# Encoder block: the operands of 336 products of 256 columns placed 64 bytes apart modulo 128

## The chip, the cores and the metric

The kernel runs on one core of one Trainium2 chip. The metric is the device time of one execution in microseconds (us); the time before is 1156.95 us, the median of three runs (1156.94 to 1157.06). Times inside an execution come from one profiled execution of the same program.

The engines that matter here are TensorE (PE in the profile; its weight loads are shown apart, as PEld), ScalarE (ACT), VectorE (DVE), GpSimd (POOL) and the queue that issues the DMAs of weights (SP). A TensorE product has a stationary operand (here always 128x128), which a weight load brings into the array, and a moving operand, whose columns are then streamed through it. Both lie in SBUF, on-chip memory of 128 partitions; "a tile begins at byte b" means byte b of every partition.

## The reference

One layer of an encoder for 256 tokens of width 2048, all in float32:

```
h = rms_norm(x, g_mix);  proj = h @ w_in          # 512 + 256 + 64 latents, and 3 x 1024 for diff attention
q = rms_norm(c_q) @ w_uq;  kv = rms_norm(c_kv) @ w_ukv          # MLA, 8 heads of 128 + 64 (rotary)
out_mla  = softmax((q_nope k_nope + q_rope k_rope) * scale) v
out_diff = rms_norm((softmax(q1 k1) - lam * softmax(q2 k2)) v)   # 4 heads, v of 256
x = x + concat(out_mla, out_diff) @ w_out
x = x + cross_attention(x, mem) @ w_xo                           # 4 heads, 256 memory tokens
x = x + (silu(hf @ w_gate) * (hf @ w_up)) @ w_down               # hidden 5632
return rms_norm(x, g_final)
```

## The kernel before

**Products in three.** Each float32 operand is held as two float32r tiles, `h` (the value rounded, written by ScalarE, line 99) and `l` (the rest, by VectorE, line 100). `mm` (lines 89 to 93) issues three products into one PSUM accumulator: h with h (line 91), h with l (92), l with h (93). In the profile the name behind the arrow lists moving and stationary operand, such as `acc<-wh,x0T_h`; buffer numbers are left out, and all three lines are shared by all products of the kernel.

**Most products have 512 columns.** A weight piece of 1 MB comes by DMA into `wraw`, is split by ScalarE and VectorE into `wh` and `wl` (4 buffers each, line 137), and is the moving operand, with a 128x128 block of the activations as the stationary one. The feed-forward part works on pairs of blocks (`wide_project`, line 680): some pairs as plain products, some as sums of blocks with seven products instead of eight; there `t24`, the last sum, has split buffers of its own, `wh2` and `wl2`, in the pool `wsum`.

**Products of 256 columns** stand in these places:

| place | moving | stationary | products |
|---|---|---|---|
| `qT`, MLA's queries by head (`stationary`, line 405, called at 427) | `cqT` | `wh`, `wl` | 96 |
| `kT`, MLA's keys by head (line 431) | `lat` | `wh`, `wl` | 48 |
| `psc`, scores of all three attentions (`scores`, line 435) | activations | activations | 168 |
| `po`, MLA's output (`heads_out`, line 477) | `pT`, the transposed probabilities | `val` | 48 |
| `po` of cross-attention (line 628) | `pxT` | `val` | 24 |
| `pod`, diff attention's output (line 531) | `val` | `pT` | 48 |
| last 512 columns of the output, in two halves (`last_mm`, line 889): k-tiles 0 to 7 | `wh`, `wl` | `hT`, `hT2`, `forms` | 96 |
| the same, k-tiles 8 to 15 (line 893) | `w_h`, `w_l`: tiles of the pool `act` | the same | 96 |

**Where the tiles lie.** The pools are stacked in the order in which they are opened, and each tile is rounded up to 32 bytes. Worked out from the tiles' sizes, `wp` (3 `wraw` of 8192 bytes, then 4 `wh` and 4 `wl` of 4096 each) begins at byte 38,400, `act` (24 tiles of 4096: all activations that are operands) at 95,744, `sb` at 194,048, `small` at 209,408 and, when the position tables are freed, `soft` at 211,200. `soft` holds `e` (the exponentials, 4 buffers of 2048), then `pT_h` and `pT_l` (2 buffers of 2048 each). `wsum` takes the place of `soft` for the feed-forward part. All these are multiples of 128, and so the moving operand of every float32r product, and the stationary operand of every one, begins at a multiple of 128 bytes. The identity matrix of the transposes lies 96 bytes past a multiple of 128 (byte 17,248). Lines 445 to 447 put the negated maxima of a softmax in `nm`, 4 buffers of 8 bytes in `small`.

**The order of the work** on each engine comes from a planner that plays the program through with a timeline of its own (line 1002); only the DMAs of weights are kept in the order of the program. Line 895 names the pool of the last weights: from the piece with k-tile 8 on they go to tiles of `act`, so that they can be ready ahead of time.

Of the kernel before, what the change touches and what calls it, by code (L numbers as in the profile page):

```python
# [11 lines left out]
F32 = mybir.dt.float32  # L12
F32R = mybir.dt.float32r
# [6 lines left out]
P = 128  # L20
S = 256
NT = S // P
# [52 lines left out]
def encoder_block(ctx: ExitStack, tc: tile.TileContext, a, out):  # L75
# [3 lines left out]
    wp = ctx.enter_context(tc.tile_pool(name="wp", bufs=3))  # L79
    act = ctx.enter_context(tc.tile_pool(name="act", bufs=24))  # L80
    sb = ctx.enter_context(tc.tile_pool(name="sb", bufs=2))
    small = ctx.enter_context(tc.tile_pool(name="small", bufs=4))
# [27 lines left out]
            act.tile(list(shape), F32R, name=name + "_l", tag="act"),  # L110
        )

    def weights(src, fine=False, pool=None, before_k=None, cut=None, raw=None):

        nk, ncols = src.shape[1:]
        begun = raw is not None
        if not begun:  # L120
            raw = wp.tile([P, 2048], F32, name="wraw", tag="wraw", bufs=3)
        raw = raw[:, :nk * ncols].rearrange("p (k c) -> p k c", k=nk)
        step = 1 if fine else nk
        for k in range(0, nk, step):
            if before_k is not None:
                before_k(k)
            if begun and k == 0:
                continue
            tc.keep_in_program_order(nc.sync.dma_start(out=raw[:, k:k + step, :], in_=src[:, k:k + step, :]))
        ks = []  # L130
        step = max(1, 1024 // ncols // 2 * 2)
        for k in range(0, nk, step):
            n = min(step, nk - k)
            if pool:
                w = pool((P, n, ncols), "w")
            else:
                w = [wp.tile([P, 1024], F32R, name=x, tag=x, bufs=4)[:, :n * ncols].rearrange("p (k c) -> p k c", k=n)
                     for x in ("wh", "wl")]
                w = Split(*w)
            if fine:  # L140
                for j in range(n):
                    for c in ([slice(0, ncols)] if cut is None or k + j else [slice(0, cut), slice(cut, ncols)]):
                        split_into(w[:, j, c], raw[:, k + j, c])
            else:
                split_into(w, raw[:, k:k + n, :])
            ks += [w[:, j, :] for j in range(n)]
        return ks
# [18 lines left out]
    def nat(name):  # L166
        return sb.tile([P, 512], F32, name=name, tag="nat", bufs=7)

    def ps_tile(name):
        return pps.tile([P, 512], F32, name=name, tag="ps")  # L170
# [73 lines left out]
    for i in range(8):  # L244
# [10 lines left out]
        for k, w in enumerate(weights(a["w_in_lat"][i], i == 0, before_k=x0T.load_one if i == 0 else None,  # L255
                                      cut=QL if i == 0 else None, raw=lat_raw if i == 0 else None)):
            xk = x0T(2 * i + k)
            for tt in range(NT):
                x = xk[:, tt * P:(tt + 1) * P]
# [77 lines left out]
    cqT = act_tile(name="cqT")  # L337
    lat = act_tile(name="lat")
    ckvT, krT = lat[:, 0:2, :], lat[:, 2:4, :]
# [45 lines left out]
    soft = soft_pool.enter_context(tc.tile_pool(name="soft", bufs=2))  # L385
# [19 lines left out]
    def stationary(wk, xT, nk, name):  # L405

        t = act_tile(name=name)
        for hp in range(2):
            ps = ps_tile(name)
            for j in range(2):  # L410
                h = hp * 2 + j
                for kt in range(nk):
                    mm(ps[:, j * S:(j + 1) * S], wk[kt][:, h * P:(h + 1) * P], xT[:, kt, :],
                       kt == 0, kt == nk - 1)
            split_into(t[:, 2 * hp:2 * hp + 2, :], ps.rearrange("p (j t) -> p j t", j=2))
        return t
# [7 lines left out]
        qrs.append(qr)  # L424
    qT, kT, vv = [], [], []
    for hg in range(2):
        qT.append(stationary(weights(a["w_uq_n"][hg]), cqT, 4, "qT"))
        if hg == 0:
            for tt in range(NT):
                transposed(qrT, qrs[tt], tt, 4)  # L430
        kT.append(stationary(weights(a["w_ukv_k"][hg]), ckvT, 2, "kT"))
        vv.append(values(project(lambda kt: ckvT[:, kt, :], [a["w_ukv_v"][hg]])))
    mla_split = last_split[0]

# [7 lines left out]

    def softmax_parts(ps, scale):

        nm = small.tile([P, NT], F32, name="nm", tag="nm", bufs=4)
        nc.vector.tensor_reduce(out=nm, in_=ps, axis=AX.X, op=ALU.max, negate=True)
        nc.vector.tensor_scalar(out=nm, in0=nm, scalar1=scale, scalar2=None, op0=ALU.mult)
        e = soft.tile([P, NT, S], F32, name="e", tag="e", bufs=4)
        ssum = small.tile([P, NT], F32, name="ssum", tag="ssum", bufs=4)
        for tt in range(NT):  # L450
            nc.scalar.activation(e[:, tt, :], ps[:, tt, :], AF.Exp, bias=nm[:, tt:tt + 1], scale=scale,
                                 accum_out=ssum[:, tt:tt + 1])
        r = small.tile([P, NT], F32, name="rs", tag="rs", bufs=4)
        nc.vector.reciprocal(out=r, in_=ssum)
        return e, r
# [128 lines left out]
    for tt in range(NT):  # L584
        n = nat("xk")
# [30 lines left out]
    for tt in range(NT):  # L616
        n = nat("xq")
# [25 lines left out]
    def w_tile(n=2, pool=None):  # L643

        pool, tags, bufs = (wp, ("wh", "wl"), 4) if pool is None else (pool, ("wh2", "wl2"), 1)
        return Split(*[pool.tile([P, 1024], F32R, name=x, tag=x, bufs=bufs)[:, :n * 512].rearrange(
            "p (b c) -> p b c", b=n) for x in tags])

    def split_blocks(src, pool=None):
# [200 lines left out]
    for gi, (chunks, order) in enumerate(groups):  # L850
# [6 lines left out]
        src = [a["w_dn"][h, pair0:pair0 + len(hp)] for h in range(2)]  # L857
# [18 lines left out]
        for oc in (2, 3):  # L876
            pieces = [a["w_down"][c, oc - 2] for c in range(len(hp) // 2)]
            if oc == 2:
                add_out(project(xT, pieces), oc)
                for tt in range(NT):  # L880
                    final(tt, oc)
                continue

            accs = [(pacc.tile([P, 512], F32, name="acc", tag="acc"), ps_tile("acc2")) for _ in range(NT)]
            n = 4 * len(pieces) - 6
            kt = 0
            ws = []

            def last_mm(tt, h, kt, w, stop):
                mm(accs[tt][h][:, :256], xT(kt)[tt], w[:, h * 256:(h + 1) * 256], kt == 0, stop)  # L890

            for p in pieces:
                for w in weights(p, pool=act_tile if kt + 4 > n else None):
                    if kt < n:
                        for tt in range(NT):
                            for h in range(2):
                                last_mm(tt, h, kt, w, False)
                    else:
                        ws.append(w)
                    kt += 1  # L900
            for tt in range(NT):
                for h in range(2):
                    for i, w in enumerate(ws):
                        last_mm(tt, h, n + i, w, i == len(ws) - 1)
                    xs = x_res[tt][:, oc * 512 + h * 256:oc * 512 + (h + 1) * 256]
                    nc.vector.tensor_tensor(out=xs, in0=xs, in1=accs[tt][h][:, :256], op=ALU.add)
                    if h == 0:
                        meansq(xs, fss[:, tt, 3:4], 256, D)
                        nc.vector.tensor_tensor(out=xs, in0=xs, in1=gfb[1][:, 512:768], op=ALU.mult)
                        nc.vector.reduce_sum(out=fss[:, tt, 5:6], in_=fss[:, tt, 0:5], axis=AX.X)  # L910
                        continue
                    sq = nat("sq")[:, :256]
                    nc.vector.tensor_tensor_reduce(out=sq, in0=xs, in1=xs, scale=1.0 / D, scalar=fss[:, tt, 5:6],
                                                   op0=ALU.mult, op1=ALU.add, accum_out=fss[:, tt, 6:7])
                rf = small.tile([P, 1], F32, name="rf", tag="rf")
                nc.gpsimd.tensor_tensor(out=rf, in0=fss[:, tt, 6:7], in1=mhalf[:, :1], op=ALU.pow)
                xr, orow = x_res[tt], out[tt * P:(tt + 1) * P, :]
                nc.vector.tensor_scalar(out=xr[:, :384], in0=xr[:, :384], scalar1=rf, scalar2=None, op0=ALU.mult)
                nc.sync.dma_start(out=orow[:, :384], in_=xr[:, :384])
                nc.scalar.activation(xr[:, 384:1152], xr[:, 384:1152], AF.Copy, scale=rf)  # L920
                nc.scalar.dma_start(out=orow[:, 384:1152], in_=xr[:, 384:1152])
                nc.vector.scalar_tensor_tensor(out=xs, in0=xs, scalar=rf, in1=gfb[1][:, 768:1024],
                                               op0=ALU.mult, op1=ALU.mult)
                nc.vector.tensor_scalar(out=xr[:, 1152:1792], in0=xr[:, 1152:1792], scalar1=rf, scalar2=None,
                                        op0=ALU.mult)
                nc.sync.dma_start(out=orow[:, 1152:], in_=xr[:, 1152:])
# [79 lines left out]
```

## Time and profile before

| | |
|---|---|
| median of three runs | 1156.95 us |
| the profiled execution | 1157.2 us, of which 1155.4 us are the span from the first to the last instruction |
| granted TensorE clock, mean | 0.998 of full speed |
| VectorE busy | 901.2 us (78%) |
| ScalarE busy | 611.4 us (53%) |
| GpSimd busy | 69.3 us (6%) |
| DMA | 222.13 MB, 192 GB/s |

How to read it: a matmul's duration in the profile runs from its first read until its result stands in PSUM, so successive ones overlap; what a product costs in a dense stretch is the distance from its start to the start of the next one, its spacing. A row of the timeline has start, duration (both us), engine, line, operation, output and operands with shapes, and the count; idle time ahead of an instruction stands in brackets with what ended it. A row of a group ends in count, busy us and the mean in ns.

### The profile page before, as it was taken

The numbers are of one execution on the slowest core, as the hardware profiler recorded it, in microseconds if no ns is written. First come the engines' busy times: TensorE is split into PE (matmuls) and PEld (weight loads), VectorE is DVE, ScalarE is ACT, GpSimd is POOL, SyncE is SP. The second block draws the span as 40 slices with busy tenths as digits, with TensorE's granted clock in tenths as the row PEclk, the third lists the DMA queues.
The fourth block names the chain that finished last, engine by engine and source line by source line (L and its number), as shares of the span: only waits on it lengthen the run. The fifth ranks groups of instructions, "written<-read, shape, count | busy, mean of one in ns | idle before, by whom it ended". The sixth has DMA issues, their size and how long they took to land.

```text
span 1155.4 us, 14401 instructions
## 1 busy us (share of the span) xinstructions
PE 1145.1 (99%) x5510; PEld 960.9 (83%) x5510; DVE 901.2 (78%) x1197; ACT 611.4 (53%) x863; POOL 69.3 (6%) x81
## 2 busy tenths in 40 slices
PE   9999999999999999999999999999999999999997
PEld 7888888888888888888888888888888888888887
DVE  6688766586867776978888787797888788798873
ACT  6755454554665555655445554554544554554552
POOL 4920000001000000000000000000000000000021
PEclk9999999999999999999999999999999999999999
DMA  9655334445754445565555555645556555555551
GB/s 343 227 207 189 126 132 165 178 146 193 283 215 173 155 146 182 182 219 182 183 198 203 193 182 207 219 169 195 192 182 222 209 183 202 195 220 204 212 202 73
DMA packets 33764, 222.13 MB, mean 192 GB/s; under 512 B 4128, under 2 KB 4896, under 8 KB 8992
## 3 DMA queue, kind: packets, MB, share of 16 engines
q1 hardware_dynamic: 32256, 216.86, 52.2%
q0 software_dynamic: 864, 3.15, 0.8%
q10 hardware_dynamic: 576, 1.21, 0.3%
q8 instruction: 43, 0.70, 0.2%
q14 instruction: 25, 0.20, 0.1%
HBM read 219.11 MB, written 2.10 MB: 191 GB/s over the span
## 4 chain that ended last, share of the span: by engine, by line
PE 98%; DMA 0%; issue 0%; DVE 0%; ACT 0%; SPq 0%; POOLq 0%; POOL 0%; DVEq 0%; ACTq 0%
PE acc L91 28%; PE acc L92 28%; PE acc L93 28%; PE q L91 2%; PE q L92 2%; PE q L93 2%; PE pt L315 2%; PE ppt L462 1%; PE psc L92 1%; PE psc L93 1%; PE psc L91 1%; DMA wraw<-in_w_in_lat 0%; PE acckv L91 0%; PE acckv L93 0%; PE acckv L92 0%; PE pt L838 0%
## 5 line engine op out<-in xcount | busy, mean ns | idle before, releaser
L99 ACT CAST wh<-wraw 128x1024 fp32r<-128x1024 f32 (+2 forms) x399 | 399.6, 1013 | 384.4 <-PE acc L93 348.0
L100 DVE TENSOR_TENSOR wl<-wraw,wh 128x1024 fp32r<-128x1024 f32 (+2 forms) x399 | 469.0, 1184 | 166.8 <-ACT wh L99 164.9
L92 PE MATMUL acc<-wl,x2n_h 128*128 128x512 f32 x480 | 185.3, 390 | 0.0
L93 PE MATMUL acc<-wh,x2n_l 128*128 128x512 f32 x480 | 185.2, 389 | 0.0
L91 PE MATMUL acc<-wh,x2n_h 128*128 128x512 f32 x480 | 160.2, 390 | 0.0
L93 PEld LDWEIGHTS acc<-wh,x2n_l 128*128 128x128 f32 x480 | 90.1, 188 | 18.7
L91 PEld LDWEIGHTS acc<-wh,x2n_h 128*128 128x128 f32 x480 | 90.1, 188 | 18.6
L92 PEld LDWEIGHTS acc<-wl,x2n_h 128*128 128x128 f32 x480 | 90.1, 188 | 18.5
L92 PE MATMUL acc<-wl,hT_h 128*128 128x512 f32 (+1 forms) x272 | 103.7, 381 | 0.0
L93 PE MATMUL acc<-wh,hT_l 128*128 128x512 f32 (+1 forms) x272 | 103.5, 380 | 0.0
L91 PE MATMUL acc<-wh,hT_h 128*128 128x512 f32 (+1 forms) x272 | 89.3, 382 | 0.0
L91 PE MATMUL acc<-wh,x0T_h 128*128 128x512 f32 x224 | 87.1, 394 | 1.6 <-ACT wh L99 0.9
L92 PE MATMUL acc<-wl,x0T_h 128*128 128x512 f32 x224 | 88.1, 394 | 0.1
L93 PE MATMUL acc<-wh,x0T_l 128*128 128x512 f32 x224 | 87.8, 393 | 0.0
L99 ACT CAST wh<-tsum 128x1024 fp32r<-128x1024 f32 x56 | 58.3, 1049 | 42.2 <-DVE tsum L712 31.1
L100 DVE TENSOR_TENSOR wl<-tsum,wh 128x1024 fp32r<-128x1024 f32 x56 | 67.9, 1220 | 9.0 <-ACT wh L99 9.0
L91 PEld LDWEIGHTS acc<-wh,hT_h 128*128 128x128 f32 x272 | 51.2, 188 | 9.8 <-issue 0.3
L93 PEld LDWEIGHTS acc<-wh,hT_l 128*128 128x128 f32 x272 | 51.2, 188 | 9.6
L92 PEld LDWEIGHTS acc<-wl,hT_h 128*128 128x128 f32 x272 | 51.2, 188 | 9.4
L91 PEld LDWEIGHTS acc<-wh,x0T_h 128*128 128x128 f32 x224 | 42.0, 188 | 10.4 <-ACT x0T_h L102 1.3
L92 PEld LDWEIGHTS acc<-wl,x0T_h 128*128 128x128 f32 x224 | 42.0, 188 | 8.2 <-DVE wl L100 0.8
L93 PEld LDWEIGHTS acc<-wh,x0T_l 128*128 128x128 f32 x224 | 42.2, 188 | 7.5
(363 smaller groups left out, 2004.8 us busy)
## 6 DMA issues: line engine op xcount, KB each, us to landing
wraw<-in_w_gu SPq DMA_DIRECT2D x80, 1024.0 KB, 4.8
wraw<-in_w_dn SPq DMA_DIRECT2D x36, 1024.0 KB, 4.8
wraw<-in_w_in SPq DMA_DIRECT2D x24, 1024.0 KB, 4.8
wraw<-in_w_out SPq DMA_DIRECT2D x16, 1024.0 KB, 4.8
wraw<-in_w_down SPq DMA_DIRECT2D x8, 1024.0 KB, 4.8
wraw<-in_w_in_lat SPq DMA_DIRECT2D x7, 832.0 KB, 7.3
wraw<-in_w_xk SPq DMA_DIRECT2D x4, 1024.0 KB, 5.7
wraw<-in_w_xq SPq DMA_DIRECT2D x4, 1024.0 KB, 4.7
```

Source lines behind the costliest of these rows:

```text
L91: nc.tensor.matmul(o, l.h, r.h, start=start, stop=False)
L92: nc.tensor.matmul(o, l.h, r.l, start=False, stop=False)
L93: nc.tensor.matmul(o, l.l, r.h, start=False, stop=stop)
L99: last_cast[0] = nc.scalar.copy(out=dst.h, in_=src).ins
L100: last_split[0] = nc.vector.tensor_tensor(out=dst.l, in0=src, in1=dst.h.bitcast(F32), op=ALU.subtract).ins
L315: nc.tensor.transpose(out=pt[:, j * P:(j + 1) * P], in_=src[:, j * P:(j + 1) * P], identity=ident)
L462: nc.tensor.transpose(out=pt[:, kt * S + tt * P:kt * S + (tt + 1) * P], in_=p[:, tt, kt * P:(kt + 1) * P], identity=ident)
```

## The change

Four edits; no instruction is added or taken away.

1. `weights` takes a new argument `skip`. The tiles `wh` and `wl` are 1056 elements long (4224 bytes, 33 times 128) instead of 1024, and the split weights begin `skip` elements into them. The same tiles in `w_tile` (and `wh2`, `wl2` there) become as long, and are used from their first element.
2. The weights for `qT` and `kT` have `skip=16`: they begin 64 bytes into their tile.
3. So have the weights of the last 512 columns, as far as they are in `wh` and `wl` (k-tiles 0 to 7). The weights in tiles of `act` (k-tiles 8 to 15) begin where they did.
4. `nm` moves from `small` to `soft`, and has 6 buffers instead of 4. Rounded up, these take 192 bytes (64 more than a multiple of 128) at the head of `soft`, ahead of `e` and `pT`.

The pools then begin at bytes 38,400 (`wp`), 96,768 (`act`), 195,072 (`sb`), 210,432 (`small`) and 212,096 (`soft`, `wsum`), all multiples of 128; `e` and `pT` begin 64 bytes past one. In the 336 products of `qT`, `kT`, MLA's `po`, `pod` and the k-tiles 0 to 7 of the last columns, moving and stationary operand are 64 bytes apart modulo 128. The other 288 products of 256 columns, and those of 512, keep both at multiples of 128.

```diff
-    def weights(src, fine=False, pool=None, before_k=None, cut=None, raw=None):
+    def weights(src, fine=False, pool=None, before_k=None, cut=None, raw=None, skip=0):
...
-                w = [wp.tile([P, 1024], F32R, name=x, tag=x, bufs=4)[:, :n * ncols].rearrange("p (k c) -> p k c", k=n)
-                     for x in ("wh", "wl")]
+                w = [wp.tile([P, 1056], F32R, name=x, tag=x, bufs=4)[:, skip:skip + n * ncols].rearrange(
+                    "p (k c) -> p k c", k=n) for x in ("wh", "wl")]
...
-        qT.append(stationary(weights(a["w_uq_n"][hg]), cqT, 4, "qT"))
+        qT.append(stationary(weights(a["w_uq_n"][hg], skip=16), cqT, 4, "qT"))
...
-        kT.append(stationary(weights(a["w_ukv_k"][hg]), ckvT, 2, "kT"))
+        kT.append(stationary(weights(a["w_ukv_k"][hg], skip=16), ckvT, 2, "kT"))
...
-        nm = small.tile([P, NT], F32, name="nm", tag="nm", bufs=4)
+        nm = soft.tile([P, NT], F32, name="nm", tag="nm", bufs=6)
...
-        return Split(*[pool.tile([P, 1024], F32R, name=x, tag=x, bufs=bufs)[:, :n * 512].rearrange(
+        return Split(*[pool.tile([P, 1056], F32R, name=x, tag=x, bufs=bufs)[:, :n * 512].rearrange(
...
-                for w in weights(p, pool=act_tile if kt + 4 > n else None):
+                for w in weights(p, pool=act_tile if kt + 4 > n else None, skip=16):
```

## The prediction

> **What bounds the kernel now.** The page first: how much of the span each engine is busy, and which engine carries the chain of work that ended last. Then the waits, to see who waits for whom.
>
> ```profile
> span 1155.4 us, 14401 instructions
> PE 1145.1 (99%) x5510; PEld 960.9 (83%) x5510; DVE 901.2 (78%) x1197; ACT 611.4 (53%) x863; POOL 69.3 (6%) x81
> PE 98%; DMA 0%; issue 0%; DVE 0%; ACT 0%; SPq 0%; POOLq 0%; POOL 0%; DVEq 0%; ACTq 0%
> ```
> ```profile
> ACT wh L99 <- PE acc L93: 359.1, 221, 7.0
> DVE nm L446 <- PE psc L93: 4.3, 4, 1.9
> ```
>
> PE is busy for 99% of the span and is 98% of the chain. ScalarE, which makes the weights, waits 359 us in total for PE to free a buffer; the supply is ahead of the products, so a product that takes less time should move what follows it forward. The change touches the spacing of products of 256 columns alone. The timeline of PE around the last columns shows that spacing beside the one at 512 columns, without a wait between them:
>
> ```profile
> 1102.06 0.39 PE L92 MATMUL acc<-wl,hT_h 128*128 128x512 f32 x1
> ...
> 1124.73 0.39 PE L93 MATMUL acc<-wh,forms_l 128*128 128x512 f32 x1
> 1124.95 0.28 PE L91 MATMUL acc<-wh,hT_h 128*128 128x256 f32 x1
> ...
> 1136.47 0.28 PE L91 MATMUL acc<-w_h,hT_h 128*128 128x256 f32 x1
> ```
>
> From 1102.06 to 1124.95 start 101 products of 512 columns: 22.89 / 101 = 226.6 ns each. From 1124.95 to 1136.47 start the 96 of 256 columns whose weights are in `wh` and `wl`: 11.52 / 96 = 120.0 ns. At the pace of the wide ones, 256 columns would take 113.3 ns. So a narrow product takes 6.7 ns more than its columns ask for. At both widths one load of 128x128 weights belongs to each product; with 256 columns it has half the time beside which to run. I take the 6.7 ns for what the load costs when it and the moving operand read the memory in step, both from a multiple of 128 bytes.
>
> **Part by part: the 336 products.** MLA's stage and the diff attention, in the same view, with the groups for the counts (one of the three lines of each):
>
> ```profile
> 72.54 0.28 PE L91 MATMUL qT<-cqT_h,wh 128*128 128x256 f32 x1
> ...
> 78.30 0.63 PE L91 MATMUL acc<-wh,lat_h 128*128 128x512 f32 x2
> ...
> 90.60 0.28 PE L91 MATMUL kT<-lat_h,wh 128*128 128x256 f32 x1
> ...
> 93.48 0.40 PE L91 MATMUL acc<-wh,lat_h 128*128 128x512 f32 x1
> ...
> 213.55 0.28 PE L91 MATMUL pod<-val_h,pT_h 128*128 128x256 f32 x1
> 213.66 0.28 PE L92 MATMUL pod<-val_l,pT_h 128*128 128x256 f32 x1
> 213.78 0.40 PE L92 MATMUL acc<-wl,x0T_h 128*128 128x512 f32 x1
> ...
> 214.71 0.28 PE L93 MATMUL pod<-val_h,pT_l 128*128 128x256 f32 x1
> ...
> 215.90 0.40 PE L93 MATMUL acc<-wh,x0T_l 128*128 128x512 f32 x1
> ```
> ```profile
> L91 PE MATMUL qT<-cqT_h,wh 128*128 128x256 f32 x32 | 9.1, 284 | 0.0
> L91 PE MATMUL kT<-lat_h,wh 128*128 128x256 f32 x16 | 4.6, 288 | 0.0
> L91 PE MATMUL po<-pT_h,val_h 128*128 128x256 f32 x16 | 4.6, 286 | 0.0
> L91 PE MATMUL pod<-val_h,pT_h 128*128 128x256 f32 x16 | 4.5, 280 | 0.0
> ```
>
> - `qT`: 48 products from 72.54 to 78.30, 120.0 ns; three lines of 32 make 96 products, 96 x 6.7 = 0.64 us.
> - `kT`: 24 from 90.60 to 93.48, 120.0 ns; 48 products, 0.32 us.
> - The last columns: 96 products, 0.64 us.
> - `pod`: ten from 214.71 to 215.90, 119 ns; 48 products, 48 x 5.7 = 0.27 us.
> - MLA's `po`: 48 products, which stand between scores and transposes. For them I take the 0.12 us that the chain gives them (next fence); 48 x 6.7 = 0.32 us.
>
> Together 2.19 us. Less goes to two things: a product that follows one of 512 columns starts its successor after 0.11 us already (213.55 to 213.66), in some 15 places, 0.1 us; and a few `po` wait for their probabilities and gain nothing, about 0.1 us. That leaves 2.0 us. The unknown is the spacing that the new place gives. Nothing in the trace shows a float32r product with its operands 64 bytes apart. The nearest rows for the lower bound are transposes:
>
> ```profile
> 119.22 0.12 PE po L93
> ...
> 400.06 1.75 PE ppt L462 x16
> ```
>
> Sixteen in 1.75 us, 109.4 ns each, with a load of 128x128 for each, and the identity that moves lies 96 bytes past a multiple of 128, its load at one. So a load can be done in 109.4 ns when the operands are not in step: the gain can reach 288 x 10.6 + 48 x 9.6 = 3.5 us. At the other end a phase can be worse than this one. After the two `pod` at 213.55 four products of 512 columns take from 213.78 to 214.71, 232.5 ns each instead of 226.6: a step out of the steady rhythm costs 5.9 ns there, and 336 x 5.9 = 2.0 us would be lost. I take 113.3 ns, the pace of the wide products, which the first narrow ones of a run already show: between the ends it is what this kernel's own float32r products reach.
>
> The Trainium skill speaks against this reading: TensorE: Matmul & The Clock Gate (Part 2, What happens when you issue a matmul) says that moving operand and weight load have independent read ports and that loading the next weights takes no read bandwidth from the running matmul. By it the operands' places do nothing and the time stays at 1156.95 us; the trace has 6.7 ns per narrow product that the columns don't explain, but cannot say that the places cause them.
>
> **What else moves.** The order of reads behind it must hold, so I look at what feeds the faster stretches. Busy time by stretch (length, then PE, PEld, DVE, ACT):
>
> ```profile
> 72.54:78.30 5.76, 5.76 (x50) 5.75 (x49) 5.76 (x14) 2.24 (x3) 0.00 (x0) 1.00 0.39 136
> 81.85:93.48 11.63, 11.63 (x100) 11.63 (x99) 9.48 (x14) 9.35 (x15) 1.47 (x2) 1.00 0.77 273
> 1124.95:1136.47 11.52, 11.52 (x98) 11.51 (x96) 6.80 (x6) 4.29 (x7) 4.39 (x2) 1.00 0.10 40
> ```
> ```profile
> 75.70 1.22 DVE L100 TENSOR_TENSOR wl<-wraw,wh 128x1024 fp32r<-128x1024 f32 x1
> ...
> 78.79 2.36 DVE L100 TENSOR_TENSOR wl<-wraw,wh 128x1024 fp32r<-128x1024 f32 x2
> ```
>
> During the first `qT` DVE is full (5.76 of 5.76 us). Its next weights are ready at 76.92, and PE asks for them at 78.30, which becomes 77.98: 1.06 us are left. Those after that are ready at 81.15; PE begins `kT` at 81.85, which becomes 81.53: 0.38 us are left. If that cover were gone, at most the 0.32 us of the first `qT` would be lost. In the other stretches DVE and ACT have 2 us and more to spare.
>
> ScalarE and VectorE write the same elements 64 bytes later: nothing, and PE's 359 us of lead cover it if not. `nm` with six buffers can only take a wait away, and its reductions wait for PE's scores alone (4.3 us, above): nothing. No instruction and no DMA is added, and no queue is passed. `e` lies 64 bytes later too, as the stationary operand of 64 transposes; the identity is then 32 instead of 96 bytes off, as far from step as before: nothing, with 64 x 6.7 = 0.4 us either way as its bounds. The planner, which does not see addresses, sees other buffers for `nm` alone; a swap of neighbours in the softmax is worth tenths of a us.
>
> The sum: 1157.2 us of the profiled execution (1155.4 of span and 1.8 around it) less 2.0 is 1155.2. The median lies 0.25 below the profiled execution, so the forecast is 1156.95 - 2.0 = **1155.0 us** (rounded).
>
> **The rivals.**
> - *No load cost remains at all.* The 336 go to the transposes' 109.4 ns, 3.5 us less: 1153.4 us. For it: the shortest spacing in the trace has operands out of step. Against it: the wide products keep 226.6 ns although their load has twice the time, so about 0.44 ns a column seems to be the stream's own pace. The skill's formula on the same page (section Back-to-back issue gap) gives N / 2.4 + 2.5 ns, 109.2 ns at 256 columns, the same as here; at 512 it gives 215.7, which the trace's 226.6 does not reach.
> - *The places don't matter.* The load with its hand-over is itself 120 ns long for float32r, and a narrow product is bound by it: 1156.95 us. For it: PEld is busy for 11.51 of the 11.52 us of the last stretch. Against it: the transposes' loads.
> - *The new phase is worse.* With 64 bytes between them load and stream meet later in each product, and the spacing settles above 120 ns, as the wide ones do at 232.5 after a disturbance: 336 x 5.9 = 2.0 us more, and with 8 ns or more, as much as 2.7: 1159.0 to 1159.7 us. It decides from 120 ns on: every ns above is 0.34 us. Against it: those 232.5 ns are passing, not steady.
> - *The wide products suffer.* Buffers of 4224 bytes put two of four `wh` and `wl` 128 bytes off a multiple of 256 from the activations. If 128 were not the whole of the pattern, half of some 4400 wide products (5510 matmuls on the page, less 624 narrow ones, 96 of 320 columns and the transposes) could take 232.5 ns: 2200 x 5.9 = 13 us, 1170 us. Against it, a stretch where the sum `t24`, in `wsum`, has its operands 256 bytes off a multiple of 512:
>
> ```profile
> 740.63 0.39 PE L91 MATMUL q<-wh,forms_h 128*128 128x512 f32 x1
> ...
> 742.67 0.84 PE L91 MATMUL acc<-wh,x2n_h 128*128 128x512 f32 x3
> ```
>
> Nine products in 2.04 us, 226.7 ns: the larger offset is free, though not the same one.
>
> **How the numbers follow.** 0.2% is 2.3 us, about what a measurement can tell from no change: faster means below 1154.6, slower above 1159.3. The chances: forecast 0.50 (its own range 1154.3 to 1155.8, from 6.7 ns a product give or take two), no load cost 0.15, places without effect 0.22, worse phase 0.08, wide products 0.05. The range leaves out the two slow cases and the far end of the best one, some 0.18: from 1153.2 to 1157.6 us. Faster: the second case and two fifths of the first, 0.35. Slower: the wide products, half of the worse phase and a remainder for the order of work, 0.11. Same: the rest, 0.54.
>
> **What would show it.** Right: the 96 products of the last columns take 10.9 us instead of 11.52, at 113 to 114 ns, while the 96 after them stay at 120.0; `qT` goes from 5.76 to 5.45 us for 48; the scores stay at 120; 512 columns stay at 226.6. Wrong in size: a spacing near 109 or 117. Wrong in mechanism: 120.0 in the last columns, or the same gain in products that did not move. The forecast fails if the wide products leave 226.6 ns, or if gaps open in front of `kT`, where the cover is thinnest.

## The result, and the profile after

| | before | changed |
|---|---|---|
| median | 1156.95 us | 1171.46 us (1170.71 to 1172.34) |
| the profiled execution's span | 1155.4 us | 1168.9 us |

The ratio is 1.0125, with a 95% interval of 1.011 to 1.0139: the change makes the kernel 14.5 us slower. The forecast was 1155.0 us, with a range of 1153.2 to 1157.6 us; it came out near the 1170 us of the fourth rival, to which the prediction gave 0.05.

The page of the changed kernel, the same three lines, and the wait that shows whether the supply still leads:

```profile
span 1168.9 us, 14401 instructions
PE 1159.8 (99%) x5510; PEld 960.3 (82%) x5510; DVE 902.0 (77%) x1197; ACT 610.9 (52%) x863; POOL 68.2 (6%) x81
PE 98%; issue 0%; DMA 0%; DVE 0%; ACT 0%; POOLq 0%; POOL 0%; DVEq 0%; ACTq 0%
```
```profile
ACT wh L99 <- PE acc L93: 374.1, 223, 7.2
```

Nothing has taken PE's place. PE is busy for 14.7 us more with the same 5510 matmuls, and the other engines have the same work as before (DVE 902.0 instead of 901.2 us). ScalarE waits longer for PE, 374 instead of 359 us: the supply leads by more. The instructions stand in the same order on every engine as before. So the products themselves are slower, and the timeline of PE around the last columns, at the same instructions that the prediction quotes, says which (start and duration in us first):

```profile
1115.61 0.40 PE L92 MATMUL acc<-wl,hT_h 128*128 128x512 f32 x1
...
1138.88 0.28 PE L91 MATMUL acc<-wh,hT_h 128*128 128x256 f32 x1
...
1149.99 0.28 PE L91 MATMUL acc<-w_h,hT_h 128*128 128x256 f32 x1
```

The 101 products of 512 columns (the wide ones, from here on) take 23.27 us, 230.4 ns each instead of 226.6. The 96 narrow ones that were moved take 11.11 us, 115.7 ns instead of 120.0: they did become faster. Joined with the place of each operand in memory, which the program fixes, the starts in the trace give for the whole kernel:

| product, distance of the moving from the stationary operand modulo 256 | before | changed |
|---|---|---|
| 512 columns, 0 | 227.2 ns (all) | 229.6 ns (some 2160) |
| 512 columns, 128 | none | 232.0 ns (some 2190) |
| `qT`, `kT` | 120 | 113 to 115 |
| last columns, 64 / 192 | 120 | 117.8 / 113.6 |
| MLA's `po`, `pod` | 119, 118 | 118.5, 117 |

(Means without waits.) The wide ones at 128 cost 2190 x 4.8 ns = 10.5 us, and the wide ones at 0, whose operands are as far apart as before, 2160 x 2.35 ns = 5.1 us more. The narrow ones give back 1.1 us. The sum, 14.5 us, is nearly the 14.7 us that PE is busy longer; the span grew by 13.5, since PE waited about 1 us less ahead of its first products of `x0T` in this execution (0.4 instead of 1.6 us).

Why those at 0 lose too can be read where the buffers alternate, at the end of the same stretch. The twelve products from 1133.35 to 1136.09 have their operands 0 apart, the twelve from there to 1138.88 have them 128 apart:

```profile
1133.35 0.39 PE L91 MATMUL acc<-wh,hT_h 128*128 128x512 f32 x1
...
1134.05 0.39 PE L91 MATMUL acc<-wh,hT_h 128*128 128x512 f32 x1
...
1136.09 0.40 PE L91 MATMUL acc<-wh,forms_h 128*128 128x512 f32 x1
```

The first three at 0 take 0.70 us, 233 ns each; the other nine take 2.04 us, 226.7 ns, the pace of the kernel before. So after a switch from 128 to 0 a few products stay slow before the pace is back. The twelve at 128 take 2.79 us, 232.5 ns each.

### The profile page after: what moved, and what is told of

Read it like the earlier page. It is cut to its first block, busy times and chain, and to the rows that moved or that the text cites. A ratio compares the mean times of both kernels' runs of the same rounds, so it can differ in the third digit from the quotient of the medians.

```text
span 1168.9 us, 14401 instructions
## 1 busy us (share of the span) xinstructions
PE 1159.8 (99%) x5510; PEld 960.3 (82%) x5510; DVE 902.0 (77%) x1197; ACT 610.9 (52%) x863; POOL 68.2 (6%) x81
## 4 chain that ended last, share of the span: by engine, by line
PE 98%; issue 0%; DMA 0%; DVE 0%; ACT 0%; POOLq 0%; POOL 0%; DVEq 0%; ACTq 0%
PE acc L91 28%; PE acc L92 28%; PE acc L93 28%; PE q L91 2%; PE q L93 2%; PE q L92 2%; PE pt L318 2%; PE ppt L465 1%; PE psc L93 1%; PE psc L91 1%; PE psc L92 1%; PE acckv L91 0%; PE acckv L92 0%; PE acckv L93 0%; PE pt L841 0%
```

## Experiments

Theory A: the wide products have a best distance of their operands, 0 modulo 256, and the buffers of 4224 bytes took half of them off it; those that stay at 0 are slowed by the neighbours that were moved. Theory B: the narrow products in their new rhythm leave the wide ones out of step. Theory C: not the distance, but the moving operand's own place counts. Each experiment stands beside runs of the kernel before on the same chip. None leaves out any work of the kernel, and every engine's instructions have the kernel's order, but for some neighbours (10 of PE's) in those with shared buffers.

**1. The narrow products alone.** `h` and `l` share a buffer that is a multiple of 256 bytes long:

```diff
-                w = [wp.tile([P, 1056], F32R, name=x, tag=x, bufs=4)[:, skip:skip + n * ncols].rearrange(
-                    "p (k c) -> p k c", k=n) for x in ("wh", "wl")]
+                t = wp.tile([P, 2112], F32R, name="wh", tag="wh", bufs=4)
+                w = [t[:, c:c + n * ncols].rearrange("p (k c) -> p k c", k=n) for c in (skip, 1024 + skip)]
...
-    first = small.tile([P, 25], F32, name="first", bufs=1)[:, :1]
+    first = small.tile([P, 57], F32, name="first", bufs=1)[:, :1]
```

(`w_tile` likewise with offsets 0 and 1024; the longer `first` brings `soft` and `wsum` to a multiple of 256.)

> The change with one thing altered: wh and wl share buffers of 8448 bytes, 33 times 256, so that the operands of every wide product stay a multiple of 256 bytes apart, while the same 336 narrow products are 64 apart. Theory A (the distance modulo 256 sets the pace of the wide products: 0 is free, 128 costs): the wide ones are back at 226.7 ns and the narrow gain stands alone, 1154.9 to 1155.2 us. Theory B (the narrow products, once they run at 114 ns, leave the wide ones out of step, whatever the places of these): 1169 to 1172 us. Theory C (the place of the moving operand by itself, modulo 256, sets the pace): as A here, 1155.

Measured: 1156.04 us beside 1156.68, ratio 0.9996 (0.9987 to 1.0005). The same three rows of the timeline:

```profile
1101.04 0.39 PE L92 MATMUL acc<-wh,hT_h 128*128 128x512 f32 x1
...
1123.93 0.28 PE L91 MATMUL acc<-wh,hT_h 128*128 128x256 f32 x1
...
1135.24 0.29 PE L91 MATMUL acc<-w_h,hT_h 128*128 128x256 f32 x1
```

The wide ones are back at 226.6 ns (22.89 / 101), while the narrow ones are at 117.8 ns (11.31 / 96). B falls: 336 faster narrow products disturb nothing. But the gain is 0.6 us in the medians, not 2, and no more than the measurement can tell from none. (All 336 are still 64 apart modulo 128, but modulo 256 not all are where the change has them: with these buffers the last columns are all at 64 and `qT` and `kT` all at 192, where the change has half of each.)

**2. The longer buffers alone.** The kernel before, with `[P, 1056]` for `[P, 1024]` in `weights`, and in `w_tile` for the pool `wp`.

> The kernel before with wh and wl in buffers of 4224 bytes and nothing else: no weights 64 bytes later, nm where it was. Theory A: half of the wide products are 128 off a multiple of 256, the narrow ones gain nothing: what the change costs plus the 2 us that its narrow products gain, 1172 to 1174 us. Theory B: nothing is out of step, 1156.9 us. Theory C: as A, since the moving operands of half the wide products begin at 128 modulo 256.

Measured: 1171.26 us beside 1156.68, ratio 1.0129 (1.0115 to 1.0143).

```profile
1115.79 0.40 PE L92 MATMUL acc<-wl,hT_h 128*128 128x512 f32 x1
...
1139.06 0.28 PE L91 MATMUL acc<-wh,hT_h 128*128 128x256 f32 x1
```

230.4 ns for the wide products (23.27 / 101), as after the whole change. The 128 bytes that each buffer was lengthened by are the whole loss; B is out.

**3 and 4. All distances, or all places.** The activations 128 bytes later, by a tile in a pool of its own ahead of `act`; then weights and activations alike 128 bytes later, by a longer tile in `const`:

```diff
+    padp = ctx.enter_context(tc.tile_pool(name="padp", bufs=1))
     act = ctx.enter_context(tc.tile_pool(name="act", bufs=24))
...
-    first = small.tile([P, 25], F32, name="first", bufs=1)[:, :1]
+    first = padp.tile([P, 32], F32, name="first")[:, :1]
```
```diff
-    mhalf = const.tile([P, 8], F32, name="mhalf")
+    mhalf = const.tile([P, 40], F32, name="mhalf")[:, :8]
```

> The kernel before with the pool of the activations 128 bytes later and wh, wl and all else where they were: every wide product has its operands 128 apart modulo 256, and none moves its moving operand. Theory A: all of some 4400 wide products take 5.4 ns more, as those 128 apart do after the change: about 1181 us. Theory B: 1156.9 us. Theory C: 1156.9 us, the moving operands being at 0 modulo 256 as before.

> The kernel before with everything, weights and activations, 128 bytes later: no distance changes, every place does. Theory A: 1156.9 us. Theory B: 1156.9 us. Theory C: all moving operands begin at 128 modulo 256, about 1181 us.

Measured: 1179.20 us (ratio 1.0195, 1.0181 to 1.0209) for the distances, 1156.39 us (0.9998, 0.9989 to 1.0007) for the places. First the timeline with all distances at 128, then with all places moved:

```profile
1123.68 0.39 PE L92 MATMUL acc<-wl,hT_h 128*128 128x512 f32 x1
...
1147.15 0.28 PE L91 MATMUL acc<-wh,hT_h 128*128 128x256 f32 x1
...
1158.53 0.28 PE L91 MATMUL acc<-w_h,hT_h 128*128 128x256 f32 x1
```
```profile
1101.44 0.39 PE L92 MATMUL acc<-wl,hT_h 128*128 128x512 f32 x1
...
1124.34 0.28 PE L91 MATMUL acc<-wh,hT_h 128*128 128x256 f32 x1
```

232.4 ns against 226.7. The distance counts, and a common shift of both operands by 128 doesn't: C is out, A holds. With all of them at 128 the kernel loses 22.5 us, so half of them alone would explain 11.3; experiment 2 lost 14.6, because those at 0 are slowed as well.

**5, 6 and 8. Other distances.** As in 3, with 64, 192 and 32 bytes (`first` of 16, 48 and 8 elements, and a longer `xss` that keeps `soft` on its grid). The question was also whether a better distance than 0 exists for the wide products.

> The kernel before with the pool of the activations 64 bytes later: every product of weights with activations has its operands 64 apart, the moving one at 192 after the stationary one modulo 256 where weights move. In the runs so far the narrow products take 113.4 ns at 192, 117.8 at 64, 118.6 at 128 and 120.0 at 0. Theory A1 (the wide ones gain in the same places as the narrow ones): they fall below 226.7 ns, to 224 perhaps, the least in the traces, 4400 x 2.7 = 12 us less: 1145 us. Theory A2 (0 is the best place of the wide ones, and every other distance costs): between 0 and the 5.4 ns of 128, near half: 1157 + 12 = 1169 us.

> The same with the activations 192 bytes later: where weights move, the moving operand is at 64 after the stationary one modulo 256. Theory A1: as the narrow ones at 64, a little better than at 0: 1152 to 1157 us. Theory A2: 1169 us, as with 64 bytes. Were 64 and 192 the same place (a pattern of 128 bytes), this run and the one with 64 bytes would be equal, and so would those with 0 and 128, which they are not.

> The kernel before with the activations 32 bytes later, the finest step of the pools: where weights move, the moving operand is at 224 after the stationary one. Theory A1: part of the gain of 64 bytes, 1150 us. Theory A2: part of its cost, 1160 to 1169 us; a pattern in lines of 64 bytes would give that cost in full or not at all.

Measured: 1182.35 us (ratio 1.0223, 1.0209 to 1.0237), 1165.21 us (1.0075, 1.006 to 1.0091) and 1182.78 us (1.0227, 1.0213 to 1.0241). The timelines of the first two:

```profile
1127.67 0.40 PE L92 MATMUL acc<-wl,hT_h 128*128 128x512 f32 x1
...
1151.23 0.28 PE L91 MATMUL acc<-wh,hT_h 128*128 128x256 f32 x1
...
1162.12 0.28 PE L91 MATMUL acc<-w_h,hT_h 128*128 128x256 f32 x1
```
```profile
1109.74 0.39 PE L92 MATMUL acc<-wl,hT_h 128*128 128x512 f32 x1
...
1132.86 0.28 PE L91 MATMUL acc<-wh,hT_h 128*128 128x256 f32 x1
```

With the moving operand 192 after the stationary one the wide products take 233.3 ns, and with 64 after it 228.9: not the same, so the pattern is not one of 128 bytes. The narrow products of the last columns take 113.4 ns (10.89 / 96) at the very distance that is among the worst for the wide ones. A1, one best place for both widths, falls. Of A2 the direction holds, since 0 is still the best place, but not the sizes: it had 1169 us for 192 and 64 alike and 1160 to 1169 us for 224. In fact 192 and 224 cost 6.7 ns a product, more than the 5.8 ns of 128, and 64 costs 2.3 ns.

**7. The last columns at 192.** Experiment 1 with `skip=48` for them instead of 16.

> The first experiment (buffers of 8448 bytes for a pair) with the last columns' weights 192 instead of 64 bytes later. Theory A, with the pattern of 256 bytes that the narrow products show (113.4 ns with the moving operand at 192 after the stationary one, 117.8 at 64): the last 96 products fall from 117.8 to 113.4 ns, 0.4 us less than the first experiment, 1155.6 us beside 1156.7 of the kernel before. With a pattern of 128 bytes, as the change assumes, nothing moves: 1156.0 us.

Measured: 1155.63 us beside 1156.41, ratio 0.9994 (0.9985 to 1.0003).

```profile
1100.69 0.39 PE L92 MATMUL acc<-wh,hT_h 128*128 128x512 f32 x1
...
1123.58 0.28 PE L91 MATMUL acc<-wh,hT_h 128*128 128x256 f32 x1
...
1134.89 0.28 PE L91 MATMUL acc<-w_h,hT_h 128*128 128x256 f32 x1
```

A miss: the median is where it was expected, but by luck, since the 96 products stayed at 117.8 ns (11.31 / 96). At the same distance, 192, they took 113.4 ns in experiment 5. So a narrow product's spacing hangs on more than its distance. The trace of experiment 1 has both spacings within one execution, in the two runs of `qT`, all of whose operands are at 192:

```profile
72.26 0.28 PE L91 MATMUL qT<-cqT_h,wh 128*128 128x256 f32 x1
...
77.92 0.40 PE L91 MATMUL acc<-wh,lat_h 128*128 128x512 f32 x1
...
84.67 0.28 PE L92 MATMUL qT<-cqT_l,wh 128*128 128x256 f32 x1
...
90.00 0.28 PE L91 MATMUL kT<-lat_h,wh 128*128 128x256 f32 x1
```

The first 48 take 5.66 us, 117.9 ns each; the last 47 of the second run take 5.33 us, 113.4 ns. In experiment 5, where `qT` is at 64, the same two stretches take 5.66 us (from 73.80) and 5.33 us (from 86.12). So 64 and 192 each have both spacings.

**9 to 12. Distances of 16, 32, 48 and 240.** Experiment 7 with the weights of the wide products later in their buffers (4, 8, 12, 60 elements), for instance

```diff
-    def weights(src, fine=False, pool=None, before_k=None, cut=None, raw=None, skip=0):
+    def weights(src, fine=False, pool=None, before_k=None, cut=None, raw=None, skip=4):
```

> Buffers of 8448 bytes for a pair, as in the first experiment, and the weights of the wide products 16 bytes into them (those in the buffers of the sums stay at 0). Wide products by distance, moving after stationary modulo 256, so far: 227.2 ns at 0, 229.2 at 64, 232.5 at 128, 233.3 at 192 and 224. Theory D1 (0 is the best place): at 16 already dearer, 228 ns or more, 1160 us or above. Theory D2 (the best place lies a little above 0, since 224 costs 6 ns and 64 only 2): below 226.7 ns, near 225, 1148 us. Theory D3 (lines of 64 bytes: where in its line an operand begins is free): 226.7 ns, 1155.6 us.

> The same with 32 bytes. Theory D1: halfway between 0 and 64, 228.2 ns, 1160 us. Theory D2: 225 to 227 ns, 1148 to 1156 us. Theory D3: 226.7 ns, 1155.6 us.

> The same with 48 bytes. Theory D1: three quarters of the way to 64, 228.7 ns, 1163 us. Theory D2: up to 228 ns, 1156 to 1160 us. Theory D3: 226.7 ns, 1155.6 us.

> The same with 240 bytes, that is 16 before the next multiple of 256. Theory D1: symmetric to 16, 228 ns or more, 1160 us or above. Theory D2: nearer to the 233.3 ns of 224 than to 0, 231 to 233 ns, 1172 to 1182 us. Theory D3: as the rest of its line, with 192 and 224: 233.3 ns, 1182 us.

Measured: 1174.69 us (ratio 1.0155, 1.014 to 1.017), 1181.04 (1.0212, 1.0197 to 1.0228), 1178.28 (1.0186, 1.0171 to 1.0201) and 1185.09 (1.0247, 1.023 to 1.0264). The timelines for 16 and for 240:

```profile
1119.98 0.40 PE L92 MATMUL acc<-wh,hT_h 128*128 128x512 f32 x1
...
1143.38 0.28 PE L91 MATMUL acc<-wh,hT_h 128*128 128x256 f32 x1
...
1154.29 0.28 PE L91 MATMUL acc<-w_h,hT_h 128*128 128x256 f32 x1
```
```profile
1129.37 0.40 PE L92 MATMUL acc<-wh,hT_h 128*128 128x512 f32 x1
...
1152.94 0.28 PE L91 MATMUL acc<-wh,hT_h 128*128 128x256 f32 x1
...
1164.24 0.28 PE L91 MATMUL acc<-w_h,hT_h 128*128 128x256 f32 x1
```

D1 holds in kind: 0 is the best of the distances tried, and 16 bytes already cost 5 ns (23.40 / 101 = 231.7); the straight line to 64 that I had drawn for 16 to 48 was far too low. Theories D2 and D3 fall. The 96 narrow products, with the same operands at the same 192 bytes in all four, take 113.6 ns behind wide ones at 16 (10.91 / 96), and 117.7 behind wide ones at 240 (11.30 / 96), as behind wide ones at 0: there are two steady rhythms at one distance. Only the place of the wide weights differs between these four kernels, which speaks for what ran ahead deciding the rhythm; but each was traced once, and whether a kernel falls into the same rhythm every time was not tried, nor why.

## Why the prediction was wrong

**The step that failed** is the first sentence on what the change reaches: "The change touches the spacing of products of 256 columns alone." It held for the edits that name those products, not for the length of the buffers that all weights share: these alone cost 14.6 us (experiment 2), because they put half of the wide products 128 off, at 232.0 ns, and slow the other half to 229.6 (both in the trace of the whole change). The fourth rival had this mechanism, its place and nearly its price, and was set aside on one stretch of the trace: products of `t24` whose operands are 256 bytes off a multiple of 512, at 226.7 ns. By the places of the operands only three of the nine products there read `t24`; but all 168 such products of the kernel before take 226.6 ns in the mean, so that the reading holds. It says that a pattern is not longer than 256 bytes; nothing in the trace spoke on 128. "The larger offset is free, though not the same one" is the place where it should have kept a larger chance than 0.05, the more since the kernel before kept every float32r product at 0 modulo 256, so that its trace could not show what a distance costs.

**The price of that rival:** 2200 x 5.9 ns = 13 us. In the trace those at 128 cost 10.5 us and those at 0 another 5.1 us, which I had not counted: a product is held up by the distance of those ahead of it as well as by its own. That 1170 us is so close to the measured 1171.46 is partly luck: 5.9 ns a product was too much (the trace has 4.8), the products at 0 were left out, and the errors partly cancel. Experiment 3, where all are at 128, gives 232.4 ns.

**The narrow products:** the direction was right, the size was not. The forecast was 6.7 ns for most of the 336, 2.0 us in all; the trace has 1.1 us. `kT` did reach 113 to 114 ns and `qT` 114 to 115; the half of the last columns at 64 stopped at 117.8, and `pod` gained 1 to 2 ns, MLA's `po` less than 1, instead of 5.7 and 6.7. The step "113.3 ns, the pace of the wide products" took one place for all 336, while "64 bytes apart modulo 128" is two places modulo 256, and neither fixes the rhythm by itself. Alone, in the places of experiment 1, the narrow part is worth 0.6 us, within the noise. The idea behind it, that operands in step cost time, fits 256 columns, where 0 is the slowest of the distances measured (120.0 ns), and has it the wrong way round for 512, where 0 is the fastest. And the 109.4 ns of the best case came from transposes, which move 128 columns (`128x128` in their rows) and not 256: they can bound the load, not a product of this width. The least steady spacing of a narrow product in any run here is 113.3 ns.

**The reading from the Trainium skill:** The Trainium skill, TensorE: Matmul & The Clock Gate (Part 2, What happens when you issue a matmul), has independent read ports for stream and load, so that loading takes no read bandwidth from the running product. Taken as a rule that the operands' places are free, as the prediction read it, the runs do not agree: a product of 512 columns takes 226.6 ns with its operands 0 apart and 233.3 ns when the activations lie 64 bytes later (experiment 5, distance 192). What in the memory or in TensorE makes the difference no run shows.

**What held:** the cover. PE remained 99% busy, no gap opened ahead of `kT`, the scores and the last 96 products stayed at 120 ns, and `nm`, `e` and the later start of the casts cost nothing that the trace shows.

## What to carry to other kernels

An edit that changes a tile's length moves every later buffer of its pool, and so every product that reads from them: list the distances of the operands of all products, not only of those that the edit names. A trace in which all operands share one distance cannot price any other, and so it can't be the ground for setting aside a rival that rests on another distance. Here 336 of 5510 matmuls were tuned, and more than 4000 others paid.

## What the runs showed of the hardware

The spacing of float32r products of 512 columns with a 128x128 load each depends on where the moving operand begins after the stationary one, modulo 256 bytes. In the trace the load that runs beside a product is that of the next one (both start at 122.29 us in the kernel before, for instance); its distance is here nearly always the same, so the runs do not say which of the two counts. The spacings are of the 101 products in the last wide stretch, one profiled execution each, the times medians of the whole kernel beside 1156.4 to 1156.7 us of the kernel before; at 16, 32, 48 and 240 the 168 products of the sums' buffers stay at 0:

| distance, bytes | spacing, ns | kernel, us |
|---|---|---|
| 0 | 226.6 | 1155.6 to 1156.4 |
| 16 | 231.7 | 1174.7 |
| 32 | 233.3 | 1181.0 |
| 48 | 233.4 | 1178.3 |
| 64 | 228.9 | 1165.2 |
| 128 | 232.4 | 1179.2 |
| 192 | 233.3 | 1182.4 |
| 224 | 233.3 | 1182.8 |
| 240 | 233.4 | 1185.1 |

A placement of 16 bytes is worth some 1.5% of this kernel (ratio 1.0155). Moving both operands by 128 changes nothing (1156.39 us). At 256 columns the best distances are others: 120.0 ns at 0, 118.5 at 128 (experiment 3, 11.38 / 96), and 113.4 or 117.8 at both 64 and 192.
